# Five tiles of a causal depthwise convolution on TensorE, four neighbouring tokens per output column

## The chip, the cores and the metric

The kernel runs on one core of one Trainium2 chip. TensorE (PE) multiplies, VectorE (DVE) and ScalarE (ACT) work elementwise and read PSUM, GpSimd (POOL) works elementwise on SBUF only, and SyncE (SP) issues nearly all DMAs from one queue, in order. The metric is the time of one execution in microseconds of device time; lower is better. The time shown is the median of three runs.

## The reference, cut to what matters

One inference step of a two-layer encoder: a Conformer convolution module, a SwiGLU FFN, an attention layer over a band of earlier chunks, and a second FFN. There are 512 prompt tokens of one new stream, whose history is zero, and 16 new tokens for each of 8 running streams, which bring 30 rows of history. The model width is 1024, and everything is f32. The change touches the convolution module alone:

```python
def conv_module(h, hist, g, w_pw1, b_pw1, w_dw, b_dw, ln_g, ln_b, w_pw2, b_pw2):
    a, gate = jnp.split(rms_norm(h, g) @ w_pw1 + b_pw1, 2, axis=-1)
    glu = a * jax.nn.sigmoid(gate)
    full = jnp.concatenate([hist.astype(glu.dtype), glu], axis=1)
    y = lax.conv_general_dilated(
        full, w_dw[:, None, :].astype(full.dtype), window_strides=(1,), padding="VALID",
        dimension_numbers=("NWC", "WIO", "NWC"), feature_group_count=D_MODEL) + b_dw
    y = jax.nn.silu(layer_norm(y, ln_g, ln_b))
    return h + y @ w_pw2 + b_pw2, full[:, -CONV_HIST:]
```

The depthwise convolution has 31 taps: each channel's output at token t is the weighted sum of that channel's values at t-30 to t. The LayerNorm behind it runs over all 1024 channels of a token, so it needs every channel's convolution before it can begin.

## The kernel before, in words

Channels lie on partitions: eight tiles c = 0 to 7 of 128 channels. The 640 tokens (128 sample tokens first, then 512 of the prompt) are two halves g = 0 and 1 of 320; half 0 holds the sample tokens and 192 of the prompt. Matrix products are made in three passes from a high and a low part of each operand (`mm3`, lines 164 to 166; weights are split by `wsplit`, lines 144 and 148).

The convolution stage is written as a list of steps, `PLAN`, which `step` carries out:

- `a`c, `b`c: `glu` of tile c for half 0 and half 1, which is two products of 24 matmuls of 320 columns, a tanh gate on ACT (lines 582 and 585), and one or two gating operations on DVE that put the result into `gall` (lines 589 and 595), one row of tokens per channel with its history ahead of it. `c`c is both with their weights and history; `C`c is both with the loads that TensorE's convolution needs. `x` is `a1` with the second half's RMSNorm in its middle.
- `d`: 31 taps on DVE for up to two pieces (`p` the 512 prompt tokens of a tile, `s` its 128 sample tokens), line 623. `q`c: the 31 prompt taps of a tile by ACT (a product, line 633) and POOL (a sum, line 636).
- `S`c, `A`c, `B`c: the convolution on TensorE (`conv_pe`, line 674) for the sample tokens, for the 192 prompt tokens of half 0, and for half 1.
- `n`g: LayerNorm of a half (`conv_ln`): column means by matmuls with a column of 1/1024 (line 199), spread over the partitions (line 211), subtraction (line 688), squares (line 171), their means, the inverse root on POOL (line 239), then scaling, Silu and the split. `w`g: the second pointwise product (`pw2`).

Tiles 0 and 3 have their prompt taps on ACT and POOL; tiles 1 and 2 on DVE; the sample taps of tiles 0 to 3 are DVE's. Tiles 4 to 7 are on TensorE. A matmul's 128 rows there are four shifts of 32 channels, its 32 output columns those channels; eight matmuls, four tokens apart, add up to 31 taps, and four column groups (q) make the 128 channels. The weights are diagonal 32x32 blocks that POOL multiplies out of a table and a folded identity (`conv_load`, line 641). The shifted copies are made by DMA: the tile's row goes to a scratch in DRAM (`conv_shift`, line 650) and comes back four times, a token further each time, onto 32 partitions each (`conv_read`, line 656). ACT brings the sum from PSUM into `y` (line 602).

What runs when: the tile framework puts every instruction on its engine's queue by list scheduling against its own cost model. Program order is the priority, moved up where the code says `high_priority`; an engine's queue is then fixed and in order, with semaphore waits between engines, and so is SP's queue of DMAs. Tiles of a pool's tag take turns in `bufs` buffers, and a new use waits until the buffer's last reader is done.

After `w1` come the first FFN (line 361 and on), the attention, and the second FFN, none of which the change touches.

## Time and profile before

| | |
|---|---|
| median of three runs | 1564.67 us (1558.76 to 1574.43) |
| the profiled execution | 1570.35 us |
| its span, first to last instruction | 1568.3 us |
| mean granted TensorE clock | 0.971 |
| PE busy | 1503.2 us (96%) |
| DVE, ACT, POOL busy | 1004.9, 674.7, 213.4 us |
| DMA moved | 164.30 MB, mean 105 GB/s |

The profile is one execution. A row of a group has the line, the engine, the operation, what it writes and reads, its shape and its count, and then the busy time in us, the mean ns of one, and the idle time before it with what ended it. A row of a timeline has start, length, engine and line; records that touch are merged. The clock is the share of TensorE's full clock that was granted. An f32 matmul leaves two records; a matmul of the high and low parts leaves one. The convolution stage, from the first matmul to the last of `w1`, is less than a fifth of the span.

### The profile page before, as it was taken

The numbers are of one execution on the slowest core, as the hardware profiler recorded it, in microseconds if no ns is written. First come the engines' busy times: TensorE is split into PE (matmuls) and PEld (weight loads), VectorE is DVE, ScalarE is ACT, GpSimd is POOL, SyncE is SP. The second block draws the span as 40 slices with busy tenths as digits, with TensorE's granted clock in tenths as the row PEclk, the third lists the DMA queues.
The fourth block names the chain that finished last, engine by engine and source line by source line (L and its number), as shares of the span: only waits on it lengthen the run. The fifth ranks groups of instructions, "written<-read, shape, count | busy, mean of one in ns | idle before, by whom it ended". The sixth has DMA issues, their size and how long they took to land.

```text
span 1568.3 us, 27283 instructions
## 1 busy us (share of the span) xinstructions
PE 1503.2 (96%) x11186; PEld 1428.8 (91%) x11186; DVE 1004.9 (64%) x1997; ACT 674.7 (43%) x1295; POOL 213.4 (14%) x239
## 2 busy tenths in 40 slices
PE   5999799999999999999999999988999999999997
PEld 5998579999999999999988788866999999999996
DVE  5788435785675575558676667563685575575555
ACT  4665145454254244246654344442444254244233
POOL 5789001000000000004221111011000000000001
PEclk9999679999999999999999999997999999999998
DMA  7256303312213222223555554351112222222211
GB/s 231 72 150 174 82 20 108 135 48 88 81 61 101 81 74 88 82 81 114 194 179 169 170 182 165 125 196 57 55 48 88 81 70 92 81 74 88 81 54 68
DMA packets 55884, 164.30 MB, mean 105 GB/s; under 512 B 10064, under 2 KB 24528, under 8 KB 47056
## 3 DMA queue, kind: packets, MB, share of 16 engines
q1 hardware_dynamic: 55472, 162.26, 32.2%
q8 instruction: 88, 1.44, 0.4%
q10 hardware_dynamic: 288, 0.31, 0.1%
q14 instruction: 36, 0.29, 0.1%
HBM read 151.13 MB, written 11.42 MB: 104 GB/s over the span
## 4 chain that ended last, share of the span: by engine, by line
PE 83%; POOL 5%; DVE 4%; ACT 3%; DMA 2%; issue 2%; POOLq 0%; SPq 0%; DVEq 0%; ACTq 0%
PE mm L361 35%; PE mm L164 13%; PE mm L166 12%; PE mm L165 12%; POOL ca L636 5%; PE w L199 2%; PE mm L674 2%; PE w L1001 1%; PE am L986 1%; PE am L1032 1%; PE am L969 1%; DMA cache<-in_ck 1%; ACT whi L144 1%; PE w L945 1%; PE w L946 1%
## 5 line engine op out<-in xcount | busy, mean ns | idle before, releaser
L361 PE MATMUL mm<-XH,wlo 128*128 128x320 f32 x736 | 228.3, 311 | 0.4 <-DVE wlo L319 0.4
L361 PE MATMUL mm<-XH,whi 128*128 128x320 f32 x736 | 227.4, 311 | 0.0
L361 PE MATMUL mm<-XL,whi 128*128 128x320 f32 x736 | 225.4, 309 | 0.0
L164 PE MATMUL mm<-xh,whi 128*128 128x320 f32 (+2 forms) x640 | 203.2, 320 | 5.9 <-ACT xh L153 4.2
L165 PE MATMUL mm<-xh,wlo 128*128 128x320 f32 (+2 forms) x640 | 202.0, 316 | 0.6 <-DVE wlo L148 0.6
L166 PE MATMUL mm<-xl,whi 128*128 128x320 f32 (+2 forms) x640 | 199.8, 316 | 0.0
L165 PE MATMUL mm<-hid,wlo 128*128 128x320 f32 (+2 forms) x560 | 171.8, 308 | 0.0
L166 PE MATMUL mm<-hid,whi 128*128 128x320 f32 (+2 forms) x560 | 169.7, 308 | 0.0
L164 PE MATMUL mm<-hid,whi 128*128 128x320 f32 (+2 forms) x560 | 167.7, 308 | 0.0
L318 ACT ACTIVATE whi<-raw 128x1536 fp32r<-128x1536 f32 (+2 forms) x90 | 101.0, 1148 | 121.3 <-PE mm L166 89.2
L319 DVE TENSOR_TENSOR wlo<-raw,whi 128x1536 fp32r<-128x1536 f32 (+2 forms) x90 | 118.7, 1340 | 40.6 <-ACT whi L318 40.4
L361 PEld LDWEIGHTS mm<-XH,wlo 128*128 128x128 f32 x736 | 139.2, 189 | 0.8 <-DVE wlo L319 0.8
L361 PEld LDWEIGHTS mm<-XH,whi 128*128 128x128 f32 x736 | 138.8, 189 | 0.0
L361 PEld LDWEIGHTS mm<-XL,whi 128*128 128x128 f32 x736 | 137.9, 188 | 0.0
L164 PEld LDWEIGHTS mm<-xh,whi 128*128 128x128 f32 x640 | 123.3, 193 | 9.9 <-ACT xh L153 4.9
L165 PEld LDWEIGHTS mm<-xh,wlo 128*128 128x128 f32 x640 | 123.6, 193 | 1.2 <-DVE wlo L148 0.8
L166 PEld LDWEIGHTS mm<-xl,whi 128*128 128x128 f32 x640 | 123.2, 194 | 1.2 <-issue 1.0
L361 PE MATMUL mm<-XH,vhi 128*128 128x320 f32 x368 | 114.2, 310 | 1.9 <-ACT XH L445 1.9
L361 PE MATMUL mm<-XH,vlo 128*128 128x320 f32 x368 | 113.8, 309 | 0.0
L361 PE MATMUL mm<-XL,vhi 128*128 128x320 f32 x368 | 113.1, 308 | 0.2
L165 PEld LDWEIGHTS mm<-hid,wlo 128*128 128x128 f32 x560 | 105.1, 188 | 0.0
L166 PEld LDWEIGHTS mm<-hid,whi 128*128 128x128 f32 x560 | 104.7, 188 | 0.0
(210 smaller groups left out, 3404.4 us busy)
## 6 DMA issues: line engine op xcount, KB each, us to landing
raw<-in_w_in SPq DMA_DIRECT2D x38, 1024.0 KB
cache<-in_ck SPq DMA_DIRECT2D x32, 512.0 KB
cache<-in_cv SPq DMA_DIRECT2D x32, 512.0 KB
raw<-in_w_pw SPq DMA_DIRECT2D x14, 1024.0 KB
raw<-in_w_out SPq DMA_DIRECT2D x18, 768.0 KB
raw<-in_w_kq SPq DMA_DIRECT2D x8, 1024.0 KB
raw<-in_w_in SPq DMA_DIRECT2D x12, 512.0 KB
raw<-in_w_out SPq DMA_DIRECT2D x12, 384.0 KB
```

Source lines behind the costliest of these rows:

```text
L144: nc.scalar.activation(out=hi[:, a:b], in_=raw[:, a:b], func=AF.Copy)
L164: nc.tensor.matmul(ps, wh, xh, start=(i == 0), stop=False)
L165: nc.tensor.matmul(ps, wl, xh, start=False, stop=False)
L166: nc.tensor.matmul(ps, wh, xl, start=False, stop=(i == last))
L199: nc.tensor.matmul(st[:, 512 + t * w + k:513 + t * w + k], s[:, a:a + P], onec, start=True, stop=True)
L318: nc.scalar.activation(out=hi[:, a:b], in_=src, func=AF.Copy)
L319: nc.vector.tensor_tensor(out=lo[:, a:b], in0=src, in1=hi[:, a:b].bitcast(F32), op=ALU.subtract)
L361: nc.tensor.matmul(pt, wt, v[x][:, k, :], start=(first and k == i == 0), stop=(k == 3 and i == 2), skip_group_check=True)
L636: nc.gpsimd.tensor_tensor(out=acc, in0=acc, in1=pr, op=ALU.add)
L674: nc.tensor.matmul(pt[32 * q:32 * q + 32, 0:n], w4[0:r, 4 * tg + q, :], mv, start=(tg == 0), stop=(tg == 7))
L945: nc.tensor.matmul(ps, QQ[:, q], KK[:, 0:n], start=True, stop=False)
L946: nc.tensor.matmul(ps, QQ[:, q], KL[:, 0:n], start=False, stop=True)
```

## The change: what it does

- **Four neighbouring tokens at once.** A matmul's 128 rows are now 16 shifts of 8 channels (four shifts `a` by DMA, four token residues `r`), and its 32 output columns are 8 channels times 4 neighbouring tokens `f`. A moving column is then a step of four tokens, so a half of 320 tokens has 80 columns. Two matmuls (`b`, four columns apart) cover 32 of the shifts. The three products that fall outside of them (tap 30 for f = 2, taps 29 and 30 for f = 3) are added afterwards on DVE.
- **Layout.** The gated values of tiles 3 to 7 lie in `g4`, split by residue: [channel, residue, step]. The gates write that layout in several operations (six for half 0, two for half 1, before two and one). The copies come back from DRAM as [8 channels x 4 residues] partitions times 16 groups of channels. `y` is kept in the order [f, step] for all tiles, so `to_y` reads and `pw2`'s last addition writes with a stride.
- **The way back.** The sums leave PSUM by a DVE addition of the bias (`ev`), go to DRAM (`ys`) and come back with the channels on partitions (`yc`); the three fix-ups follow (six operations for half 0, three for half 1).
- **Five tiles.** Tile 3 moves to TensorE. Tile 2's prompt taps move from DVE to ACT and POOL; DVE keeps tile 1's prompt taps and the sample taps of tiles 0 to 2.
- **Weight tables.** POOL makes each table of 1024 columns in four operations of 256 (`conv_w`), once for each half, into two buffers instead of three: ten tables instead of four.
- **The plan.** The first halves of tiles 3 to 7 (`G`) go ahead of `n0`; all second halves (`H`) go behind it, and so does the pointwise product of tile 5's second half, whose weights are loaded and split a second time (`W5`).
- **LayerNorm sums.** Squares are summed by DVE (half 0) or POOL (half 1) before the column sums instead of on PE (`rstd_bc` with a cut of 8 instead of 1), and half 1's means are summed on POOL over all eight tiles (before: six).

The host makes the new tables and reorders the history and the returned convolution state; TensorE's part of the diff and the plan:

```diff
-LNO = ((0, 1, 4, 2, 5, 3, 6, 7), (0, 1, 4, 2, 5, 3, 6, 7))
-PLAN = ("a0 y x1 b0 b1 q0 dp1s0 c2 ds1p2 c3 C4 q3 ds2s3 C5 S4 A4 B4 C6 S5 A5 C7 S6 A6 S7 A7 n0 B5 L7 B6 "
-        "B7 s0 n1 w0 w1")
+LNO = ((0, 1, 3, 4, 5, 2, 6, 7), (0, 1, 2, 3, 4, 6, 7, 5))
+PLAN = ("a0 y x1 b0 b1 q0 W2 W3 a2 b2 dp1s0 k3 a3 W4 b3 X3 q2 ds1s2 k4 a4 G3 k5 W5 b4 X4 a5 G4 k6 W6 a6 W7 a7 "
+        "G5 Y7 k7 b6 W5 G6 k3 b7 W8 G7 n0 k4 H3 X6 k6 H4 X7 k7 b5 H6 X5 k5 H7 H5 s0 n1 w0 w1")
...
+        sc = dr.tile([P, 4, w], F32, tag=f"s{g}", name=nm("sc"), bufs=3 if g == 0 else NC4)
+        nc.sync.dma_start(sc, gc[:, :, k0:k0 + w])
+        scs[c, g] = sc
+        if g == 0:
+            if c < 7:
+                shift(c, 0)
+            nc.sync.dma_start(convs4_out[:, c - C0], gc[:, :, 0:NS4])
+
+    def shift(c, g):
+        w = (WG, WH)[g] - 3
+        x4 = cp.tile([P, 16, w], F32, tag=f"x{g}", name=nm("x4"), bufs=2)
+        src = scs[c, g].rearrange("(z c) r w -> (c r) z w", c=8)
+        for a in range(4):
+            nc.sync.dma_start(x4[32 * a:32 * a + 32], src[:, :, a:a + w])
+        x4s[c, g] = x4
...
+    def conv_w(c):
+        w4 = w4t().rearrange("p (b c f) -> p b c f", c=8, f=4)
+        i = V_DW4 + 128 * (c - C0)
+        for f in range(4):
+            nc.gpsimd.tensor_tensor(
+                out=w4[:, :, :, f], in0=i8[:, None, :].to_broadcast([P, 32, 8]),
+                in1=dwv[:, i + f:i + 128:4].unsqueeze(2).to_broadcast([P, 32, 8]), op=ALU.mult)
+        w4s.append(w4)
+
+    def conv_pe(c, g):
+        w4, x4 = w4s.pop(0), x4s.pop((c, g))
+        gc, i = g4[:, c - C0], c - C0
         pt = mmt()
...
+        parts = ((0, KG, 0),) if g else ((0, KS, None), (KS, KA, NS4))
+        for rr in range(4):
+            for o, n, k in parts:
+                for b in range(2):
+                    for q in range(4):
+                        z = 4 * rr + q
...
+                        nc.tensor.matmul(pt[32 * q:32 * q + 32, rr * KG + o:rr * KG + o + n],
+                                         w4[:, 2 * z + b].rearrange("p c f -> p (c f)"), mv,
+                                         start=(b == 0), stop=(b == 1), skip_group_check=True)
+        with tc.high_priority(offset=HP):
+            ev = cp.tile([P, 4, KG], F32, tag="ev", name=nm("ev"), bufs=2)
...
+            ys = dr.tile([P * 4, KG], F32, tag="ys", name=nm("ys"), bufs=4)
+            nc.sync.dma_start(ys.rearrange("(r p) k -> p r k", p=P), ev)
+            yc = y[g][:, c, :]
+            nc.sync.dma_start(yc, ys.rearrange("(p f) k -> p (f k)", f=4))
+            yf = yc.rearrange("p (f k) -> p f k", f=4)
+            for f, r, j in ((2, 0, W - 1), (3, 0, W - 2), (3, 1, W - 1)):
+                for o, n, k in parts:
...
+                    nc.vector.scalar_tensor_tensor(out=out, in0=src, scalar=dcol(V_DW + c * W + j),
+                                                   in1=out, op0=ALU.mult, op1=ALU.add)
...
-        r, v = colmean(mu, [lambda c=c: y[g][:, c, :] for c in order], n, LCUT if g else 0, "mst")
+        r, v = colmean(mu, [lambda c=c: y[g][:, c, :] for c in order], n, KT if g else 0, "mst")
...
-        bc, _ = rstd_bc([y[g][:, c, :] for c in order], n, SQ, 1)
+        bc, _ = rstd_bc([y[g][:, c, :] for c in order], n, SQ, KT, None,
+                        nc.gpsimd if g else nc.vector)
```

More of the change, by code (lines that the diff above doesn't have):

```diff
@@ L547, in tile_trunk @@
     nc.gpsimd.memset(gp[:, :, HIST + T:], 0.0)
+    g4 = cp.tile([P, NC4, 4, L4], F32, name="g4", tag="g4")
+    for i in range(NC4):
+        nc.gpsimd.memset(g4[:, i, :, NS4:NS4 + 8], 0.0)
+        nc.gpsimd.memset(g4[:, i, 2:4, L4 - 1:L4], 0.0)
     i4 = cst.tile([P, 32], F32, name="i4", tag="i4")
@@ L601, in to_y @@
             if u < v:
-                nc.scalar.activation(out=y[g][:, c, u - g * NH:v - g * NH], in_=src[:, u - o:v - o],
-                                     **kw)
+                ku, kv = (u - g * NH) // 4, (v - g * NH) // 4
+                nc.scalar.activation(
+                    out=y[g][:, c, :].rearrange("p (f k) -> p f k", f=4)[:, :, ku:kv],
+                    in_=perm(src[:, u - o:v - o]), **kw)
     def taps(c, part, j):
```

196 lines of the change are left out of this document (108 added, 88 removed).

## The prediction, made before the changed kernel was built or run

> **What bounds the kernel now.** I read the page first: the engine line and the chain of waits.
>
> ```profile
> span 1568.3 us, 27283 instructions
> PE 1503.2 (96%) x11186; PEld 1428.8 (91%) x11186; DVE 1004.9 (64%) x1997; ACT 674.7 (43%) x1295; POOL 213.4 (14%) x239
> PE 83%; POOL 5%; DVE 4%; ACT 3%; DMA 2%; issue 2%; POOLq 0%; SPq 0%; DVEq 0%; ACTq 0%
> ```
>
> TensorE is busy for 96% of the span and carries 83% of the chain. POOL's 5% is odd for an engine that works 14% of the time: its additions lie in the convolution stage, the only one that the change touches. So I cut that stage into stretches (columns: length; busy time and instructions of PE, weight loads, DVE, ACT, POOL; granted clock; DMA share; GB/s), and then took ten-microsecond pieces.
>
> ```profile
> 18.00:160.00 142.00, 136.36 (x1212) 129.46 (x1216) 113.90 (x217) 82.66 (x135) 114.61 (x81) 1.00 0.48 134
> 160.00:178.00 18.00, 7.68 (x152) 5.74 (x144) 13.56 (x34) 2.53 (x7) 0.00 (x0) 0.72 0.81 159
> 178.00:223.00 45.00, 42.43 (x351) 30.22 (x351) 11.57 (x32) 11.11 (x22) 2.59 (x3) 0.80 0.07 17
> 223.00:290.00 67.00, 67.00 (x422) 67.00 (x422) 36.21 (x54) 35.89 (x55) 8.04 (x7) 0.88 0.32 107
> ...
> 70.00:80.00 10.00, 10.00 (x70) 10.00 (x70) 8.57 (x14) 6.84 (x10) 9.53 (x7) 1.00 0.32 107
> 220.00:230.00 10.00, 10.00 (x44) 10.00 (x44) 5.03 (x12) 7.73 (x17) 0.00 (x0) 0.50 0.01 2
> 230.00:240.00 10.00, 10.00 (x44) 10.00 (x43) 0.55 (x1) 0.85 (x2) 0.00 (x0) 0.54 0.00 0
> ```
>
> Four regimes. To 160 us PE is dense at full clock: 70 matmuls in 10 us, so 0.143 us for a 128x320 one. From 160 to 178 it works 7.7 of 18 us. From 178 to 223 it is called busy, but the clock is 0.80 and the work is small. From 223 on it is dense again, the first 17 us at half clock (44 instead of 70 in 10 us). The timelines of PE, then of DVE and POOL, say what ends each regime.
>
> ```profile
> 155.55 1.96 PE L674 MATMUL mm<-xa,w 128*32 128x128 f32 x64
> 158.13 2.81 PE L674 MATMUL mm<-xa,w 128*32 128x192 f32 x64 [0.63 <-ACT t L582]
> 169.94 6.73 PE L674 MATMUL mm<-xa,w 128*32 128x128 f32 x128 [8.99 <-DMA xa<-sa]
> 178.34 2.17 PE L199 MATMUL w<-onec,y 128*128 128x1 f32 x18 [1.67 <-issue]
> 204.42 2.36 PE L674 MATMUL mm<-xb,w 128*32 128x320 f32 x32
> 219.04 4.00 PE L199 MATMUL w<-onec,sq 128*128 128x1 f32 x18 [0.66 <-ACT sq L171]
> 222.90 0.61 PE L166 MATMUL mm<-xl,whi 128*128 128x320 f32 x1
> 292.69 0.83 PE L199 MATMUL w<-onec,acc 128*128 128x1 f32 x6 [0.19 <-ACT bcw L432]
> ```
>
> ```profile
> 155.63 1.28 POOL L636 TENSOR_TENSOR ca<-ca,cvt 128x512 f32<-128x512 f32 x1
> 167.97 6.62 DVE L623 SCALAR_TENSOR_TENSOR w<-gall,dwv,w 128x128 f32<-128x128 f32 x17
> 195.95 3.27 DVE L688 TENSOR_TENSOR y<-y,w 128x320 f32<-128x320 f32 x8 [5.95 <-PE w L211]
> 212.19 0.18 DVE L203 TENSOR_REDUCE rst<-w 128x3 f32<-128x24 f32 x1 [12.97 <-PE w L199]
> ```
>
> The LayerNorm of the first half (`n0`) begins at 178.3, when two things end together: tile 7's S and A parts (176.7, after 9 us for its shifted copies) and DVE's taps of tile 3 (174.6). POOL had ended at 156.9. From there 44.6 us pass until the pointwise product `w0` runs at 222.9, and `w0` and `w1` end at 292.7. The stage is thus a front (to 178), a LayerNorm chain that PE's own queue slows down (178 to 223), and a dense tail.
>
> **The change part by part.** *The convolution matmuls.* A record of the trace is half an f32 matmul, so 64 records are the 32 matmuls of a part. At 128, 192 and 320 columns a record costs 1.96/64 = 31 ns, 2.81/64 = 44 and 2.36/32 = 74: linear, about 0.22 ns a column, and at 80, 48 and 32 columns the line gives 20, 14 and 10. The smallest column-group matmuls of the trace have 64 columns:
>
> ```profile
> 765.77 0.29 PE L1004 MATMUL w<-kt,qbd 128*32 128x64 f32 x8
> ```
>
> Eight records in 0.29 us, the last of them some 0.2 us long, start about 10 ns apart. But these are a burst of eight; in 128 on end the weight loads may set the pace, with the 128-column rate of 31 ns as the upper bound. I take 20 ns. A first half is 128 records, a second half 64: 2.6 and 1.3 us (bounds 1.5 to 3.9, and 1.3 to 2.0). Before, a tile cost 1.96 + 2.81 + 64 x 0.074 = 9.5. Five tiles at 3.9 against four at 9.5: 19 us less on PE.
>
> The Trainium skill ("TensorE: Matmul & The Clock Gate", section "Wait — 56ns, not 53.3ns?") puts a floor of about 25 ns between starts, however narrow the matmul; by it a first half is 3.2 us and the sum below 3 us longer, and the burst above (10 ns) does not agree with it.
>
> *The other engines of the front.*
>
> ```profile
> L623 DVE SCALAR_TENSOR_TENSOR w<-gall,dwv,w 128x512 f32<-128x512 f32 x60 | 42.8, 745 | 0.2
> L623 DVE SCALAR_TENSOR_TENSOR w<-gall,dwv,w 128x128 f32<-128x128 f32 x120 | 39.3, 349 | 1.8
> L148 DVE TENSOR_TENSOR wlo<-raw,whi 128x2048 fp32r<-128x2048 f32 x14 | 35.5, 2539 | 9.1 <-ACT whi L144 9.0
> L589 DVE SCALAR_TENSOR_TENSOR gall<-t,t 128x128 f32<-128x128 f32 x8 | 2.4, 305 | 15.7 <-ACT t L582 15.7
> L190 DVE TENSOR_TENSOR acc<-acc,sq 128x320 f32<-128x320 f32 x10 | 4.9, 490 | 1.8 <-ACT sq L171 1.6
> ...
> L636 POOL TENSOR_TENSOR ca<-ca,cvt 128x512 f32<-128x512 f32 x60 | 91.5, 1526 | 16.6 <-ACT cvt L633 8.0 <-ACT ca L633 4.4
> L641 POOL TENSOR_TENSOR w<-i,dwv 128x1024 f32<-128x1024 f32 x4 | 8.9, 2225 | 3.2 <-DVE xl L154 3.2
> L190 POOL TENSOR_TENSOR acc<-acc,y 128x320 f32<-128x320 f32 x4 | 3.5, 869 | 41.0 <-ACT y L602 40.9
> L549 POOL TENSOR_TENSOR i<-ident 128x32 f32<-128x32 f32 x1 | 0.3, 252 | 0.0
> ```
>
> DVE loses tile 2's prompt taps (31 x 0.745 = 23.1) and tile 3's sample taps (31 x 0.349 = 10.8). It gains, for five first halves, an eviction (0.49 by the 320-column addition), six fix-ups and four more gates each; these have 32 to 96 columns, between 0.18 (the reduce above) and 0.305 (128 columns), taken as 0.25. With one more weight split, 2.5: 5 x (0.5 + 1.5 + 1.0) + 2.5 = 17.5. So its taps end about 16 us earlier than 174.6, near 158.
>
> POOL keeps two tiles of taps. A weight table is now four operations of 256 columns; between 0.252 (32 columns) and 0.869 (320) a line gives 0.73, so 2.9 a table (bounds 2.2, today's single operation, and 3.5). Two tables can be made before the taps begin, as three of today's were; four come before the taps' end: 12 us, in place of one table (2.2) and three additions of `n1` (2.6). The end moves from 156.9 to about 164 (161 to 166), and tile 2 waits for it.
>
> *The front on PE.* By 155.5 PE has done all pointwise products and 4.77 + 9.5 = 14.3 of convolution. After: 155.5 - 14.3 - 6.9 (tile 5's second half goes behind `n0`: 48 x 0.143) + 5 x 2.6 = 147.3, if its copies are there. They take a trip through DRAM, as today's do. The SP queue shows it, timeline first, then SP's waits (total, times, longest):
>
> ```profile
> 158.88 0.56 SPq L650 DMA_DIRECT2D sa<-gall  x1
> 161.68 1.74 SPq L656 DMA_DIRECT2D xa<-sa  x4
> ```
>
> ```profile
> SPq L656 <- DMA sb<-gall: 16.8, 4, 6.1
> SPq L656 <- DMA sa<-gall: 16.2, 4, 8.7
> ```
>
> From the write's issue (158.88) to the matmul that it releases (169.94) it is 11.1 us with a wait of 2.8 between; with the mean wait (4.05) 12.3, with the longest 17. Ahead of it lie eviction and six gates, 2.2. So 14.5, or 19.2 at the worst, against a cover of two half tiles and a conv group, 2 x 6.9 + 2.6 = 16.4. The bytes are today's in four times as many pieces, which no row prices: nothing to a few us a trip. I take two late trips of 4 us, and 3 us for the clock behind them (it was 0.72 in 160 to 178): the last first-half group ends at 158.
>
> New behind it is y's own trip: eviction 0.5, two waits of 4.05, issues 0.8, fix-ups 1.5, in all 11 (bounds 8 and 19). Tile 7's y is there at **169**, after POOL's 164: `n0` begins there, not at 178.3.
>
> *The LayerNorm chain.* Squares are now summed on DVE (`n0`) or POOL (`n1`) instead of by matmuls, 21 matmuls fewer in each half and 6 fewer for `n1`'s mean. They are these rows:
>
> ```profile
> L199 PE MATMUL w<-onec,sq 128*128 128x1 f32 x120 | 18.9, 283 | 1.4 <-ACT sq L171 1.4
> L199 PE MATMUL w<-onec,y 128*128 128x1 f32 x60 | 10.2, 302 | 1.7 <-issue 1.7
> ...
> L171 ACT ACTIVATE sq<-y 128x320 f32<-128x320 f32 x16 | 7.5, 467 | 32.7 <-DVE y L688 20.2 <-PE w L199 10.3 <-issue 2.1
> L696 ACT ACTIVATE n<-y,vec 128x320 f32<-128x320 f32 x16 | 10.1, 646 | 9.0 <-DVE y L694 5.7 <-DVE xl L154 3.3
> ```
>
> 96 records go, 0.12 us each at full clock (2.17/18): 11.5 us, more at half clock. And the squares stop waiting for PE (10.3 us), whose queue held B parts between them. The chain after: the last tile's mean, its spread and one conv group ahead in PE's queue, 4; eight subtractions 3.27 and seven additions of 0.49, 6.7; from the reduce to `w0` today 222.9 - 212.2 = 10.7, less `n1`'s eight subtractions, which stood in between, 7.4. In all 18: `w0` starts at **187**. Five second halves and tile 5's product (13.4 us of PE) fill that time at no cost; without it they would follow and cost themselves.
>
> *The tail.* 384 matmuls x 0.143 = 54.9; `n1`'s remaining 12 records and spreads 2.4; the first product waits for eight tiles of z, 7 x (0.65 + 0.47) - 24 x 0.143 = 4.4 (the split's activation taken as long as a square); half clock at the start. Today it lasts through 220 to 240 with PE busy throughout, but with `n1`'s column sums strewn in (the group at 219.0 is the first), and loses (1 - 44/70) x 20 = 7.4. With those gone I take half, 3.7. Sum 65.4: **252.5**. By the Trainium skill (the same page, "What's actually happening") one busy window of about 3.4 us restores the clock; the 20 us above do not agree, and by that rule the start would cost 1.7 and the sum be 2 us less.
>
> Tile 5's second half comes last of all: product, trip, group, trip, then `n1`'s chain. Product at 167, 14.5 and 11 of trips and a short group give 194, `n1` with z for all tiles 26 more, 220, against `w0`'s end at 223. Bounds 0 and 16 (both trips at their longest, 5 + 8, less the 3 of slack, and POOL's seven additions of 0.87 in a row); I take 3.
>
> The stage ends at 255.5 instead of 292.7: 37 us less. The profiled execution took 1570.35 (span and 2 around it), so 1533; it stands 5.7 above the median of the three runs, so against the median **1528**. With all lower bounds `n0` starts at 161 (POOL's), `w0` at 179, and a tail without half clock (61.7) ends at 241: 1513. With all upper ones, 154 + 20 of late trips + 19, 18, 70 and 16, the stage ends at 297, no gain.
>
> **The rivals.** *The copies starve PE.* DMA share is 0.48 on average in the front and 0.81 at its end, and the change adds a tile and y's trips to one in-order queue, where reads that wait for a write hold up what follows. If each of five trips takes the longest (19.2, a miss of 3 to 4 with the clock lost behind it) and y's trip 19, `n0` starts at 147 + 5 x 5.5 + 19 = 194, 25 later than forecast: gain 12, **1552**. For it the 8.7; against it the mean of 4.05.
>
> *Weight tables behind the taps.* In program order tile 2's taps stand before the tables of tiles 4 to 7. If POOL keeps that order, groups 5 to 7 wait until 164; three tables, three groups, y's trip: 164 + 9 + 3 + 11 = 187, 18 later, **1546**. Against it: a table was made amid the taps before.
>
> *`n1` comes late* by its whole 16, and PE falls to half clock before `w1` (7.4): 20 more, **1548**.
>
> *Slower: DVE stands still for y.* The fix-ups wait on DVE for y to land; behind them in its queue are the gates that feed the next trip, the weight splits and the taps. If a round trip takes the two longest waits, 8.7 + 6.1 = 14.8, five of them are 74 us of standing; DVE has 169 - 158 = 11 to spare. It decides from (11 + 37)/5 = 9.6 us a visit; at 14.8 the front is 63 later, 26 slower than now: **1591**. Against it: it needs every trip to be at its worst and the queue order to put the fix-ups first.
>
> **How the numbers follow.** Forecast 0.54 (own range 1513 to 1545), starved copies 0.15, tables 0.12, `n1` late 0.09, DVE standing 0.10. The range reaches from 1512 to 1562: it leaves out the DVE rival and half of the starved case's upper side. One per cent, about what a measurement tells from no change, is 1549 to 1580. Faster: nearly all of the forecast (0.52), 0.06 of the copies, 0.10 of the tables, 0.05 of `n1`: 0.73. Slower 0.11, the DVE rival and a little of the copies; same 0.16.
>
> **What would show it.** First-half groups of 128 records in about 2.6 us; the first column sums of y at 165 to 175; no stretch below full clock longer than 7 us between that and `w1`; `w0` about 18 us behind them; POOL's last tap near 164; PE's FFN sums near 255. The forecast fails if PE waits for copies at most groups, if DVE's longest idle time is for y, or if `w1` starts more than 35 us behind `w0`.

## The result and the profile after

The changed kernel takes 1575.27 us (median), the kernel before 1558.80 in runs beside it on the same chip: a ratio of 1.0085, 95% interval 1.0059 to 1.0111. It is slower by 0.85%, where the forecast was 2.3% faster (1528 against 1564.67). The profiled execution took 1576.21 us, against 1570.35 before. Executions of one kernel spread by some 20 us, the longer ones at a lower mean clock (1552.0 us at 0.985 to 1574.1 at 0.968 for the kernel before, beside a later run), and the profiled one of the kernel before lies 11.5 us above its median, that of the changed kernel 0.9: so the two traces show 6 us where the medians show 16.5.

The page, in the order in which it was read before: the span, the engines, and the chain of waits by engine.

```profile
span 1574.4 us, 27608 instructions
PE 1473.0 (94%) x11282; PEld 1414.4 (90%) x11282; DVE 1019.5 (65%) x2020; ACT 671.0 (43%) x1281; POOL 241.4 (15%) x297
PE 78%; DVE 9%; DMA 6%; ACT 2%; POOL 2%; issue 2%; SPq 1%; POOLq 0%; DVEq 0%; ACTq 0%
```

TensorE works 30 us less, as the forecast had it (19 and 11.5), and the span is 6.1 us longer. In the chain PE loses five points; DVE goes from 4% to 9%, DMA from 2% to 6%. The stretches of the convolution stage (length; busy time and instructions of PE, weight loads, DVE, ACT, POOL; granted clock; DMA share; GB/s):

```profile
18.00:160.00 142.00, 118.21 (x1214) 116.21 (x1214) 104.12 (x221) 72.10 (x114) 104.15 (x86) 0.92 0.61 143
160.00:198.00 38.00, 25.87 (x373) 24.71 (x371) 21.28 (x26) 11.69 (x16) 23.64 (x25) 0.77 0.65 150
198.00:225.00 27.00, 13.72 (x223) 12.52 (x222) 17.77 (x48) 6.03 (x12) 7.57 (x10) 0.63 0.68 139
225.00:298.00 73.00, 66.54 (x433) 65.43 (x434) 47.72 (x70) 39.14 (x65) 18.00 (x17) 0.93 0.33 107
```

No engine is busy through the two middle stretches, 65 us long: PE 40 us, DVE 39, POOL 31. What passes there is the time of a chain. The timeline of PE shows its links on PE's side (start, length, engine, line, operation; in brackets the idle time before and what ended it): the five first-half groups, the last column sums, and the first matmul of `w0`.

```profile
96.24 2.37 PE L716 MATMUL mm<-x,w 128*32 128x32 f32 x128 [7.53 <-DMA x<-sc]
120.22 2.36 PE L716 MATMUL mm<-x,w 128*32 128x32 f32 x128 [5.71 <-DMA x<-sc]
146.57 2.36 PE L716 MATMUL mm<-x,w 128*32 128x32 f32 x128 [8.12 <-DMA x<-sc]
158.04 1.42 PE L716 MATMUL mm<-x,w 128*32 128x32 f32 x128
169.04 1.41 PE L716 MATMUL mm<-x,w 128*32 128x32 f32 x128 [2.34 <-issue]
...
197.45 4.00 PE L205 MATMUL w<-onec,y 128*128 128x1 f32 x18
...
225.45 0.64 PE L170 MATMUL mm<-xh,whi 128*128 128x320 f32 x1 [2.31 <-ACT xh L159]
```

The groups themselves are cheaper than forecast, but three of five wait for their copies, and the last ends at 170.5. SP's queue shows the trip of tile 5's copies, the write and the first two of four reads:

```profile
125.51 0.52 SPq L631 DMA_DIRECT2D sc<-g  x1
135.70 0.86 SPq L643 DMA_DIRECT2D x<-sc  x2
```

From the write's issue to the group at 146.57 it is 21.1 us; for tiles 3 and 4 (writes at 83.95 and 101.41) it is 12.3 and 18.8. From the last group's end to `w0` it is another 55 us. The timeline of DVE says why:

```profile
159.95 2.32 DVE L739 SCALAR_TENSOR_TENSOR y<-g,dwv,y 128x32 f32<-128x32 f32 x4 [9.95 <-DMA y<-ys]
162.19 3.06 DVE L603 SCALAR_TENSOR_TENSOR g<-t,t 128x160 f32<-128x160 f32 x2
165.17 1.47 DVE L739 SCALAR_TENSOR_TENSOR y<-g,dwv,y 128x32 f32<-128x32 f32 x2
166.57 3.35 DVE L154 TENSOR_TENSOR wlo<-raw,whi 128x2048 fp32r<-128x2048 f32 x1
169.84 0.48 DVE L721 TENSOR_TENSOR ev<-mm,dwv 128x320 f32<-128x320 f32 x1
170.24 1.95 DVE L603 SCALAR_TENSOR_TENSOR g<-t,t 128x160 f32<-128x160 f32 x2
179.07 5.03 DVE L739 SCALAR_TENSOR_TENSOR y<-g,dwv,y 128x32 f32<-128x32 f32 x6 [6.87 <-DMA y<-ys]
184.02 2.28 DVE L154 TENSOR_TENSOR wlo<-raw,whi 128x2048 fp32r<-128x2048 f32 x1
186.22 0.88 DVE L721 TENSOR_TENSOR ev<-mm,dwv 128x320 f32<-128x320 f32 x2
192.65 0.49 DVE L721 TENSOR_TENSOR ev<-mm,dwv 128x320 f32<-128x320 f32 x1 [5.55 <-DMA ys<-ev]
197.43 1.11 DVE L739 SCALAR_TENSOR_TENSOR y<-g,dwv,y 128x32 f32<-128x32 f32 x6 [4.29 <-DMA y<-ys]
```

The fix-ups at 159.95 and 165.17 are tile 5's. The eviction at 169.84 is tile 6's, the fix-ups at 179.07 are tile 6's, and only behind them and a weight split stands tile 7's eviction (186.22), 15.8 us after its group. Tile 7's y comes back at 197.4 and is complete at **198.5**, where the forecast had 169. Two trips through DRAM that could overlap stand one behind the other, because DVE's queue is in order and the fix-ups wait in it. From 198.5 it is 26.9 us to `w0` and 72.7 from there to the last matmul of `w1` (298.1, before 292.5).

The waits between 60 and 310 us (total, times, longest) carry both trips:

```profile
DVE y L739 <- DMA y<-ys: 31.9, 8, 9.9
PE mm L716 <- DMA x<-sc: 31.8, 5, 8.1
```

### The profile page after: what moved, and what is told of

The parts are those of the page before. It is cut to its first block, busy times and chain, and to the rows that moved or that the text cites. A ratio compares the mean times of both kernels' runs of the same rounds, so it can differ in the third digit from the quotient of the medians.

```text
span 1574.4 us, 27608 instructions
## 1 busy us (share of the span) xinstructions
PE 1473.0 (94%) x11282; PEld 1414.4 (90%) x11282; DVE 1019.5 (65%) x2020; ACT 671.0 (43%) x1281; POOL 241.4 (15%) x297
## 4 chain that ended last, share of the span: by engine, by line
PE 78%; DVE 9%; DMA 6%; ACT 2%; POOL 2%; issue 2%; SPq 1%; POOLq 0%; DVEq 0%; ACTq 0%
PE mm L367 35%; PE mm L170 12%; PE mm L171 12%; PE mm L172 12%; DMA cache<-in_ck 2%; DVE wlo L154 1%; DMA ys<-ev 1%; PE w L1057 1%; DVE w L676 1%; PE am L1042 1%; DMA sc<-g 1%; POOL ca L689 1%; PE am L1025 1%; DVE g L603 1%; PE am L1088 1%
## 5 line engine op out<-in xcount | busy, mean ns | idle before, releaser
L170 PEld LDWEIGHTS mm<-xh,whi 128*128 128x128 f32 x640 | 124.9, 196 | 14.8 <-ACT xh L159 6.4
```

What stands on the lines that cost most here:

```text
L170: nc.tensor.matmul(ps, wh, xh, start=(i == 0), stop=False)
```

## The experiments

Times are medians; a ratio is to the kernel before in the same runs, with its 95% interval, and differences to the changed kernel are taken from the ratios (1.0085 for the changed kernel; 1% is 15.6 us). In the texts on record H and G are second and first halves, b5 is tile 5's second product, and "sums" are the column sums of `n0`.

**The two trips, taken away.** First y's way back (`ev` is written into `y` at its place on chip, in the wrong order):

```diff
+            yc = y[g][:, c, :]
-                out=ev, in0=pt[:, 0:4 * KG].rearrange("p (r k) -> p r k", r=4),
+                out=yc.rearrange("p (r k) -> p r k", r=4), in0=pt[:, 0:4 * KG].rearrange("p (r k) -> p r k", r=4),
-            nc.sync.dma_start(ys.rearrange("(r p) k -> p r k", p=P), ev)
-            nc.sync.dma_start(yc, ys.rearrange("(p f) k -> p (f k)", f=4))
```

> The changed kernel, but the sums go from PSUM straight into y: no ys, no yc, no wait for them (channels and tokens of y then stand in the wrong order, so what it computes from there on is not the reference's; the operations and their sizes are the same). Theory A (PE starved by the x copies; it stood 31.8 us for x<-sc in the changed kernel): y's trip matters little, at most 10 us less than the changed kernel, 1565 or more. Theory B (DVE standing for y, 31.9 us in 8 waits, 9.9 the longest, with gates and weight splits queued behind): 25 to 35 us less, 1540 to 1550. Theory C (both are one loop: gates, copy, group, y, gates): 15 to 25 less.

Measured 1554.06, ratio 0.9929 (0.9906 to 0.9951): 24 us less than the changed kernel. Then the wait of the copies for their own write, by reading tile 3's scratch for every tile (with five scratch buffers instead of three, so that it stays):

```diff
-        src = scs[c, g].rearrange("(z c) r w -> (c r) z w", c=8)
+        src = scs[C0, g].rearrange("(z c) r w -> (c r) z w", c=8)
```

> The changed kernel, but the shifted copies of every tile are read from tile 3's scratch, so that a read never waits for its own tile's write (all writes stay, all bytes stay; tiles 4 to 7 are convolved from tile 3's values, which is not the reference). Theory A: PE's 31.8 us for x<-sc go, with the half clock behind them: 25 to 35 less than the changed kernel, 1540 to 1550. Theory B: 10 less at most. Theory C: 15 to 25 less.

Measured 1556.16, 0.9959 (0.9925 to 0.9994): 20 us less. Both edits:

> Both edits at once (wrong order in y and tile 3's values for tiles 4 to 7). If the two trips are all that the forecast missed, this gives the forecast's time, 1528 with n0 near 165. If strided gates, the tables on POOL or the LayerNorm chain cost much by themselves, it stays above 1540.

Measured 1549.90, 0.9916 (0.9879 to 0.9953): 26 us less, not 44. The two trips are links of one loop: gates, write, copies, group, eviction, trip, fix-ups, and on DVE the next gates. Each edit shortens the other trip's wait too: PE's for copies falls from 31.8 to 25.6 us without y's trip, DVE's for y from 31.9 to 19.8 without the copies' wait. That the gains do not add has a second reason, the next bound. Without y's trip alone tile 7's y is complete at 173.9, and the column sums wait for the taps that POOL adds up, until 184.7; with both trips gone they wait for ACT's copy of the same taps, and POOL's last addition ends at 179:

```profile
179.74 3.43 PE L205 MATMUL w<-onec,y 128*128 128x1 f32 x18 [1.45 <-ACT y L654]
```

So POOL was the next bound to test: the same kernel, and the five weight tables of the second halves not made (the second halves use tile 7's).

```diff
+            made.append(c)
+            if len(made) <= NC4:
+                conv_w(c)
```

> The kernel without both trips (e3), and without the five tables of the second halves, which use the table of tile 7 instead (not the reference). There POOL's taps ended at 179 and n0 began at 179.7. If POOL is what bounds it then: five tables of 2.6 us and more fewer, n0 begins near 168 and the time falls by 8 to 12 from e3, to about 1540. If not, it stays at 1550.

Measured 1543.33, 0.9884 (0.982 to 0.9949). That is 5 us below the run with both edits by the ratios, whose intervals overlap. The last column sums move to 170.5, within 2 us of the forecast's 169:

```profile
170.51 4.00 PE L205 MATMUL w<-onec,y 128*128 128x1 f32 x18 [0.68 <-ACT y L654]
```

But `w0` starts at 198.2, not 187: from the complete y (170.1) it is still 28.0 us, where the forecast had 18. That part is left to the second halves, below.

**The LayerNorm sums.** The kernel before with the change's sums alone (the two lines of `conv_ln` in the diff):

> The kernel before with one part of the change alone: squares of the LayerNorm summed by DVE (first half) and POOL (second half), the second half's means on POOL over eight tiles. The forecast's chain: 178 to 223 becomes some 25 to 30 us long and the half clock in w0 shorter, 12 to 20 us less than the kernel before. If PE's queue was not what slowed that chain: within 5 us of the kernel before.

Measured 1548.02, 0.9897 (0.9853 to 0.9942): the sums are worth 1%, and this kernel beats both. It starts `w0` at 203.5, the changed one at 225.5. The converse, the changed kernel with the sums of before:

> The changed kernel with its LayerNorm sums put back as before (squares by PE's column sums, half 1's means over six tiles on POOL and the rest on PE). Alone on the kernel before, that part gave 13 to 15 us. If the parts add up, this is some 13 to 15 us slower than the changed kernel, near 1589, and the convolution's part alone costs 25 us and more. If the LayerNorm part was spent by the trips (PE waits anyway), it is within 5 us of the changed kernel.

Measured 1581.36, 1.0119 (1.0063 to 1.0176): only 5 us over the changed kernel. That does not mean that the sums are worth less here: in this trace tile 7's y is complete at 190.7, 7.8 us earlier than in the changed kernel, and yet `w0` starts at 229.0, 3.5 us later. From y to `w0` it is 38.3 us instead of 26.9, so the old sums cost 11 us in the chain, and the earlier y hides most of it. What the convolution's part of the change costs follows from the first of the two runs: 1.0085 against 0.9897, some 29 us.

**The second halves.** Tile 5's second product back in its place ahead of `n0` (in `PLAN`, `b5` behind `W6`, no second `W5`; `b6` ahead of and `a7` behind `G5`):

> The changed kernel with the plan's move undone: tile 5's second half is made in its place, between G4 and a6, its weights are loaded once, and G5 to G7 come later in program order. Theory C (a loop of trips, with PE covering 15 us of each): the cover of G5 and G6 grows by 6.9 us, PE's wait for copies falls from 31.8 to about 18, and no second-half product stands before the last column sums: 8 to 15 less than the changed kernel, 1560 to 1567. If POOL's tables and taps set the start of n0 (they ended at 184 there): within 5 us of the changed kernel.

Measured 1570.21, 1.0063 (1.003 to 1.0096), 3 us less, which the intervals do not separate from none. PE's wait for copies falls to 25.9 us, not to the 18 expected, DVE's wait for y grows to 43.5, and tile 7's y is complete at 198.4, as before. Then the order on PE alone: the second halves and `b5` queued behind `n0`'s last column sums.

```diff
+        if lasts and tok[0] in "Hb":
+            with tc.issue_after(lasts[0]):
+                step(tok[0], tok[1:])
```

> The changed kernel, with one edge more in PE's queue: the second halves and the pointwise product of tile 5's second half stand behind the last column sums of the first half, not ahead of them. Everything is computed as in the changed kernel. Theory A (the work that the prediction let fill the LayerNorm's time at no cost was put ahead of its first step, and held it up): tile 7's y and the last taps are ready at about 184, so the last column sums start at 184 to 187 instead of 197.5, the product w0 at 212 to 216 instead of 225.5, and the time falls by 8 to 12 us to 1563 to 1567. Theory B (that work only filled time; something else, such as the weight split or the additions behind it, sets the end): the sums start earlier but w0 and w1 do not, and the time stays within 3 us of 1575. Theory C (tile 5's second half is now later by its 7 us and the second LayerNorm with it): w0 starts earlier, but PE stands before w1, and the time is 1573 to 1580.

Measured 1571.07, 1.0042 (1.0011 to 1.0072): 7 us by the ratios, 4 by the medians, less than theory A gave. Its premise was misread: the fix-ups that end at 184 are tile 6's, as shown above; tile 7's y was not ready. In this kernel y is complete at 190.5, 8 us earlier, although DVE does the same things in the same order from tile 5's fix-ups to tile 7's eviction:

```profile
158.45 0.77 DVE L741 SCALAR_TENSOR_TENSOR y<-g,dwv,y 128x32 f32<-128x32 f32 x4 [9.78 <-DMA y<-ys]
159.14 0.80 DVE L605 SCALAR_TENSOR_TENSOR g<-t,t 128x160 f32<-128x160 f32 x2
159.86 1.32 DVE L741 SCALAR_TENSOR_TENSOR y<-g,dwv,y 128x32 f32<-128x32 f32 x2
161.10 2.79 DVE L154 TENSOR_TENSOR wlo<-raw,whi 128x2048 fp32r<-128x2048 f32 x1
```

From y's landing to tile 6's eviction it is 5.4 us here (the eviction starts at 163.81) and 9.9 in the changed kernel: there all of these operations fall beside POOL's, here the first four fix-ups fall into a pause of POOL. What that does to them is told below. The start of `w0`, 222.1, is only 3.4 us earlier: the second halves now stand behind the sums and stretch the way to `w0` from 26.9 to 31.5. The decisive run leaves them out (one second table and the second split of tile 5's weights stay):

```diff
-"... G7 n0 k4 H3 X6 k6 H4 X7 k7 b5 H6 X5 k5 H7 H5 s0 n1 w0 w1"
+"... G7 n0 H s0 n1 w0 w1"   (H: zeros into that half of y and of g4)
```

> The changed kernel without the second halves on TensorE: behind the first LayerNorm's start in program order nothing is left of the second halves of tiles 3 to 7 (no second tables after the first, no copies back, no groups, no trips of y, no product of tile 5's second half, 48 matmuls or 6.9 us); that half of y and the part of tile 5's history that it would have written are filled with zeros by POOL. The first halves and their trips are as in the changed kernel. What is left out is the work that the prediction let fill the LayerNorm's time at no cost. If it does cost nothing but its place ahead of the column sums: sums at 184 to 187, then the 28 us that the changed kernel needs from its sums to the product w0, so w0 at 212 to 215, and 1560 to 1564. If it also stretches the LayerNorm chain by standing in the in-order queues of DVE, ACT and SP: from the sums to w0 it is 18 to 22 us, w0 at 204 to 208, and the time is 1550 to 1555, since nothing is late before w1 either. If the second halves are not what holds the column sums: sums at 195 or later, and 1568 to 1575.

Measured 1550.59, 0.9927 (0.9893 to 0.9962): 24.6 us less than the changed kernel. Its DVE and PE timelines:

```profile
177.84 0.48 DVE L721 TENSOR_TENSOR ev<-mm,dwv 128x320 f32<-128x320 f32 x1
179.47 2.83 DVE L739 SCALAR_TENSOR_TENSOR y<-g,dwv,y 128x32 f32<-128x32 f32 x6 [1.15 <-DMA y<-ys]
187.53 1.11 DVE L739 SCALAR_TENSOR_TENSOR y<-g,dwv,y 128x32 f32<-128x32 f32 x6 [5.23 <-DMA y<-ys]
```

```profile
199.79 1.44 PE L205 MATMUL w<-onec,acc 128*128 128x1 f32 x6 [8.13 <-DVE acc L196]
203.05 1.65 PE L217 MATMUL w<-ident,rst 128*128 128x128 f32 x6 [1.81 <-POOL rst L245]
206.87 0.64 PE L170 MATMUL mm<-xh,whi 128*128 128x320 f32 x1 [2.17 <-ACT xh L159]
```

Tile 7's y is complete at 188.6, and from there to `w0` it is 18.2 us; the forecast said 18. With the second halves it was 198.5 and 26.9. The difference is 9.9 us ahead of the column sums, 8.7 in the chain and 5.5 in the tail (`w0` to the end of `w1` is 67.2 against 72.7): 24.1 together, about what was measured. Not all of it is the second halves' own work: here the planner has put tile 7's eviction (177.84) ahead of tile 6's fix-ups (179.47), and that order alone gives 9.5 us with the second halves in place, as the run on the order shows below. What lies behind the complete y, 14.2 us, is theirs as far as the traces show. How they cost 8.7 us in the chain stands in the changed kernel's DVE timeline: squares' sums of `n0` queued behind an eviction that waits for its buffer.

```profile
210.35 2.28 DVE L196 TENSOR_TENSOR acc<-acc,sq 128x320 f32<-128x320 f32 x4 [0.54 <-ACT sq L177]
216.69 0.49 DVE L721 TENSOR_TENSOR ev<-mm,dwv 128x320 f32<-128x320 f32 x1 [4.06 <-DMA ys<-ev]
217.10 1.08 DVE L196 TENSOR_TENSOR acc<-acc,sq 128x320 f32<-128x320 f32 x2
```

**Who issues the writes.** Both trips' writes from ACT's queue in place of SP's:

```diff
-        nc.sync.dma_start(sc, gc[:, :, k0:k0 + w])
+        nc.scalar.dma_start(sc, gc[:, :, k0:k0 + w])
-            nc.sync.dma_start(ys.rearrange("(r p) k -> p r k", p=P), ev)
+            nc.scalar.dma_start(ys.rearrange("(r p) k -> p r k", p=P), ev)
```

> The changed kernel with the writes of both trips (sc and ys) issued from ACT's queue instead of SP's, so that they don't stand behind reads and weight loads that were issued before them. If the place in one queue makes the trips long (a write of 300 KB took 9.1 us at 101.4, with four reads and a weight load ahead of it): SP's waits for sc and ys fall from 57 to about 30 us, 10 to 18 less than the changed kernel, 1557 to 1565. If the DMA engines' total work makes them long: no change beyond 5 us.

Measured 1562.79, 1.0016 (0.9987 to 1.0046): 11 us less than the changed kernel. Each write alone:

> The changed kernel; only the write that sends a tile's gated values to the scratch (ahead of the shifted copies) is issued from ACT's queue, the write of the sums stays on SP's. With both on ACT's queue the time was 1562.8, about 12 us under the changed kernel. If that gain came from the copies (their write no longer stands behind other transfers in SP's queue), this kernel takes 1562 to 1566, and PE's waits for copies fall from 32 us to about 21. If it came from y's trip, this kernel stays at 1572 to 1577, and DVE still waits about 30 us for y.

> The changed kernel; only the write of the sums to DRAM (the first leg of y's trip) is issued from ACT's queue. If y's trip made the gain of the two writes together: 1562 to 1566, and DVE's wait for y falls from 32 us to 15 to 20. If the copies made it: 1572 to 1577. If each carries half, both this kernel and the one with only the other write take 1567 to 1571.

The copies' write alone: 1565.08, 1.0026 (0.999 to 1.0062), 9 of the 11 us. The sums' write alone: 1571.59, 1.0063 (1.003 to 1.0096), little or nothing, although there tile 7's y is complete at 190.0 and `w0` starts at 215.4, 10 us earlier than in the changed kernel. Its tail takes 75.3 us instead of 72.7, at a mean granted clock of 0.90 instead of 0.93, and the execution profiled is 3 us under the median of its ten. But the gain of the copies' write does not come as expected, through the copies. With their write on ACT's queue PE waits for copies as long as before, and DVE's wait for y is what fell (from 31.9):

```profile
PE mm L716 <- DMA x<-sc: 31.2, 4, 9.6
DVE y L739 <- DMA y<-ys: 17.1, 7, 4.3
```

There tile 6's eviction stands ahead of tile 5's fix-ups (161.3 against 165.3; in the changed kernel behind them, 169.8 and 160.0), and tile 7's y is complete at 190.6. A new order of DVE's queue came with the edit; whether the queue of the write itself gives anything is not separated. Combinations did not add:

> The changed kernel with two edits at once that were made alone before: the writes of the trips are issued from ACT's queue instead of SP's (alone 1562.8, about 12 us less), and tile 5's second half is back in its place ahead of the first LayerNorm (alone 1570.2, about 5 us less). If they are two causes that add up: 1558, a ratio to the kernel before of 0.998. If both only made the same thing earlier (fewer waits in SP's one queue while the copies are due): 1562 to 1565, no better than the first alone. If the extra cover for the copies makes them on time altogether, more than the sum: below 1555, with PE's waits for copies under 15 us (21 and 26 us with the edits alone, 32 without).

> The changed kernel with both writes on ACT's queue (alone 1562.8) and with the second halves' work behind the last column sums of the first half on PE (alone 1571.1). If the two losses are in series, the trips before the column sums and the planner's order at them, the gains add up: 1558 to 1559. If the sums in the kernel with both writes wait for something else than the order (there ACT's copy of the taps into y, which stands 13 us behind the issue of a write on ACT), the order gives nothing: 1562 to 1566. Neither theory takes it below the kernel before with the new LayerNorm sums alone (1548.0): for that the tables and taps on POOL, which end at 184, would have to end earlier.

The writes with tile 5's product in its place: 1572.76, 1.0051 (1.0018 to 1.0084). With the sums first: 1571.31, 1.0057 (1.0026 to 1.0088). In the first, tile 7's y is complete at 200.3, as late as in the changed kernel; in the second at 187.6, but `w0` starts 32.7 us behind it.

**The order on DVE, by itself.** A first half's fix-ups are queued behind the next first half's eviction:

```diff
+        if g == 0:
+            if late:
+                with tc.issue_after(evi.ins):
+                    late.pop()()
+            late.append(fix)
+            if c == KT - 1:
+                late.pop()()
```

> The changed kernel with one change of order on DVE: the six fix-ups of a first half, which wait for that tile's y to come back, are queued behind the next first half's eviction instead of ahead of it (tile 7's own stand behind its own eviction, as before). Everything is computed as in the changed kernel. In the changed kernel's trace tile 7's group ends on PE at 170.5, its eviction starts at 186.2, behind tile 6's fix-ups that wait 6.9 us for y, and its fix-ups end at 198.6. Theory A (the trips of y stand one behind the other in DVE's in-order queue): tile 7's eviction starts at 173 to 177, its fix-ups end at 186 to 189, w0 starts 8 to 12 us earlier, at 213 to 217, and the time falls to 1562 to 1567. Theory B (the fix-ups' place changes nothing, because DVE waits for the same landing a little later and the gates behind it with it): tile 7's fix-ups end at 195 or later and the time stays within 3 us of 1575.

Measured 1564.36, 1.0015 (0.9982 to 1.0048): 11 us less than the changed kernel, with every operation still there. DVE's timeline:

```profile
173.40 0.48 DVE L721 TENSOR_TENSOR ev<-mm,dwv 128x320 f32<-128x320 f32 x1
174.98 4.17 DVE L742 SCALAR_TENSOR_TENSOR y<-g,dwv,y 128x32 f32<-128x32 f32 x6 [1.10 <-DMA y<-ys]
...
187.91 1.11 DVE L742 SCALAR_TENSOR_TENSOR y<-g,dwv,y 128x32 f32<-128x32 f32 x6 [4.23 <-DMA y<-ys]
```

Tile 7's eviction now starts 3.6 us behind its group (169.8), the wait for tile 6's y is 1.1 instead of 6.9, and y is complete at 189.0; `w0` starts at 215.4, 10 us earlier. In the stage DVE waits 7.8 us for y instead of 31.9, and PE 20.7 for copies instead of 31.8. Theory A stands for the trips. What the order is worth in time is less certain than the 11 us: the run with the sums' write alone has its y and its `w0` as early and gains 3 (the intervals of the two overlap), and the execution profiled here, the slowest of ten, loses half of the 10 us again in its tail (77.6 us at a mean clock of 0.86). With the copies' write on ACT's queue as well:

> The same change of order, and the write that sends the gated values to the scratch issued from ACT's queue (alone 1565.1; there tile 7's fix-ups already ended at 190.6). If both act through the same thing, the time at which tile 7's y is complete, the sum cannot be had: 1561 to 1566. If the write's place acts through the copies and the order through y, they add up: 1554 to 1558, with tile 7's y complete at 182 or earlier and POOL's taps (184) the last before the column sums.

Measured 1563.97, 1.0015 (0.998 to 1.005), nothing more, although in its trace tile 7's y is complete at 183.0. The column sums then wait for ACT's copy of POOL's taps (183.5), and `w0` comes 31.5 us later, at 215.0: what was won ahead of the sums is lost behind them, to the second halves.

**One try for more.** The kernel before with the new LayerNorm sums, and its copies' write on ACT's queue:

> The kernel before with the LayerNorm sums of the change (alone 1548.0), and the writes of its shifted copies issued from ACT's queue instead of SP's. If the place of the write in SP's queue is what PE waits for (9.1 us for tile 7's copies at 168), the wait falls to 2 to 5 us and the time to 1541 to 1545. If the wait is the trip itself, through DRAM and back, it stays at 8 to 9 us and the time at 1546 to 1549. If the issue stands behind ACT's own work (a product of taps takes it most of a microsecond, an activation 0.5), the copies are later, and the time is 1550 to 1555.

Measured 1551.05, 0.989 (0.9829 to 0.9951), no better than without that edit (0.9897); tile 7's wait for copies is 10.5 us there, against 9.1.

## Why the prediction was wrong

The forecast for the profiled execution was 1533 us; it took 1576.2. The forecast for the end of the stage was 255.5; it is 298.1, which is nearly the same gap. (Against the medians it is 47 us: the forecast took 5.7 off for the median, and the changed kernel's profiled execution lies only 0.9 above its own.) The 42.6 us between are 29.5 until tile 7's y is complete, 8.9 in the chain to `w0` and 4.2 in the tail.

**"Tile 7's y is there at 169": 29.5 us.** The last group ends at 170.5 instead of 158 (12.4): "two late trips of 4 us" were three of 7.5, 5.7 and 8.1 us, because from a tile's product to its group 14.5 us were taken, 2.2 for gates and 12.3 for the copies. For tiles 3, 4 and 5 it took 9.3, 12.7 and 11.0 from the product's end to the write's issue: the tanh waits in ACT's queue for tiles 3 and 4, the gates in DVE's, tile 5's behind tile 3's fix-ups, which wait 7.4 us for y. From the write's issue to the group it took 12.3, 18.8 and 21.1; the reads of tiles 4 and 5 were issued only 9.1 and 10.2 us behind the write, against 2.8 in the row that the forecast started from. Whether the smaller pieces, which the forecast put at nothing to a few us, or the other transfers make it so long, no run separates. Then y's trip was priced alone, "in all 11", as if DVE were free: eviction to fix-ups is indeed 12.3 (186.2 to 198.5), but the eviction itself came 15.8 late, behind tile 6's fix-ups and a split. The mechanism was in the prediction, as the rival "DVE stands still for y", and was weighed at 0.10 by a price of 14.8 us a visit that no visit has: DVE waits 31.9 us in 8 visits, 4.0 each. It does not take the price to decide: what counts is that one visit stands in front of the next trip. The experiments on the trips and on the order show this, in the times of y and `w0` more firmly than in the total.

**"Fill that time at no cost": 14 us.** The second halves and tile 5's product were costed by PE's free time. They also use DVE, SP and two `ev` buffers, in order, amid the LayerNorm's own operations. Without them the chain is 18.2 us (forecast 18) and the tail 67.2 (forecast 65.4 and 3); with them 26.9 and 72.7. Even with both trips gone and five tables fewer the chain takes 28.0. That 18.2 meets 18 so closely is partly luck: the forecast took 222.9 for the start of `w0` before, but that row is where `w0` goes on behind `n1`'s column sums; its first 8 of 192 matmuls had run from 216.95.

```profile
216.95 0.42 PE L164 MATMUL mm<-xh,whi 128*128 128x320 f32 x1 [1.57 <-ACT xh L153]
```

By that row the last piece of the forecast's sum is 4.8 us instead of 7.4. Without the second halves it takes 5.6 (201.27 to 206.87, at half clock), and the column sums of the squares, which the sum left out, 1.5.

**"Taken as 0.25": right alone, wrong beside POOL.** The same six fix-ups take 1.11 us at 197.43 and 5.03 at 179.07, in the DVE rows above. The same six gates of a first half, in two rows of DVE's timeline, and POOL's additions of that time:

```profile
133.66 5.13 DVE L603 SCALAR_TENSOR_TENSOR g<-t,t 128x32 f32<-128x32 f32 x6
145.96 1.06 DVE L603 SCALAR_TENSOR_TENSOR g<-t,t 128x32 f32<-128x32 f32 x6
```

```profile
125.73 15.56 POOL L689 TENSOR_TENSOR ca<-ca,cvt 128x512 f32<-128x512 f32 x10
149.03 1.31 POOL L696 TENSOR_TENSOR w<-i,dwv 128x256 f32<-128x256 f32 x2 [7.73 <-PE mm L716]
```

The first set falls into a run of POOL additions, the second into POOL's pause from 141.3 to 149. A single gate of 32 columns takes 0.20 us or 1.34, and the excess is at most the rest of the POOL operation that runs (1.26 to 1.3 each). Added up over the gates and fix-ups between 75 and 185 us it is 21 us of DVE's time. Much of DVE's time there is idle, so not all of it counts; on the way from tile 5's y to tile 6's eviction it makes the difference between the 9.9 us and the 5.4 above. No run takes it away by itself. The Trainium skill ("SBUF — State Buffer", section "SBUF: two separate sides") says that a DVE operation with two SBUF inputs and a GpSimd operation that reads SBUF exclude each other for a whole instruction. These rows agree. So does the eviction, which reads PSUM and takes 0.48 to 0.51 throughout, and so do DVE's tap operations of 512 columns, whose running sum lies in PSUM (a tile of the pool `w2`): 0.747 us on the mean beside POOL and 0.761 without. The prediction took its durations from wide operations and left this rule out. The groups of the whole kernel (busy us, mean ns):

```profile
L603 DVE SCALAR_TENSOR_TENSOR g<-t,t 128x32 f32<-128x32 f32 x20 | 8.7, 477 | 1.1 <-ACT t L596 1.1
L739 DVE SCALAR_TENSOR_TENSOR y<-g,dwv,y 128x32 f32<-128x32 f32 x15 | 8.1, 540 | 30.1 <-DMA y<-ys 30.1
L696 POOL TENSOR_TENSOR w<-i,dwv 128x256 f32<-128x256 f32 x40 | 29.2, 771 | 38.9 <-PE mm L716 34.2 <-DVE xl L160 4.5
```

**"Four come before the taps' end": 184, not 164.** A table costs 4 x 0.771 = 3.1 us, as forecast (2.9), but seven of the ten fell among the taps, not four. They also waited in POOL's queue: with two buffers a table waits for the group that reads the one before it, 5.3 us at 122.7 and 7.7 at 149.0 (the <-PE of the group above), and the taps wait behind it. So PE's late groups reach POOL as well. It did not decide here, since y came later still; it is the bound as soon as y is early.

**What was right.** The record pace: 1.41 us for 128 records at full clock, 11 ns each and 22 a matmul, below the value taken (20 a record) and near the burst of eight (10), while the floor of 25 ns in the Trainium skill ("TensorE: Matmul & The Clock Gate", section "Wait — 56ns, not 53.3ns?") doesn't hold for these. The LayerNorm sums (16 us on the kernel before, where 11.5 and more were expected of the column sums that go). The length of the tail, once nothing else is in its queues, and that of the chain with the luck said above. Of the signs of a failure that it named, all three came: PE waits for copies at three of the five first groups, DVE's longest idle time in the stage (9.9) is for y, and `w1` starts 39.5 us behind `w0` (265.0).

## What to carry to other kernels

An operation that waits for a round trip through memory, queued on an in-order engine, delays whatever the next round trip needs of that engine: put the next trip's first step ahead of the last trip's final step, or the trips run one after the other. Work that fills a gap on one engine is free only if it is free on every engine and buffer that it passes; cost it on each, and take it out in one run to see. Small elementwise operations that read SBUF twice are priced beside what POOL runs at that time, not by their width.

## What the runs showed of the hardware that was not expected

- A DVE operation of 0.20 us that reads SBUF twice can take 1.34 when POOL works on SBUF, nearly seven times as long. The cost runs both ways. Of POOL's tap additions, the 13 that lie beside DVE's taps alone, which read SBUF once and PSUM once, take 1.27 to 1.31 us, like the 12 with nothing beside them (1.27 to 1.30); those that lie beside a weight split of 2048 columns, which reads SBUF twice, take up to 3.2. The latter make most of the excess in their mean of 1.487.
- The second product's addition with a stride of 16 bytes (line 779) takes 806 ns where the contiguous one (line 714 before) took 546, with or without POOL.
- In the changed kernel the granted clock came back 3.0 to 5.9 us after PE took up dense work: the products run at half rate from 225.45 to 228.5, and behind the groups at 96.24, 120.22 and 146.57 the full rate is back at 102.2, 126.1 and 150.0. Before, in its one profiled execution, the products of `w0` ran at half rate for 16 us and more (to 239.3). The Trainium skill's window of 3.4 us ("TensorE: Matmul & The Clock Gate", section "What's actually happening") is in line with the changed kernel, since it runs freely and work can begin in its midst, and not with the kernel before. The column sums strewn among the products there are suspect: in the kernel before with the new sums the half rate ends 5.3 us after `w0` starts. But in the execution profiled with the fix-ups queued behind, 21.5 us of the tail are at half rate without them, so the cause stays open.
